# Six of the eight w_ob blocks ahead of the attention's combination, and the column sums of the second LayerNorm's mean in other stages

## The chip, the core and the metric

The kernel runs on one core of a Trainium2 chip. The metric is the device time of one execution in microseconds (us). Five engines take part. TensorE (PE in the profile; its weight loads are PEld) multiplies matrices. VectorE (DVE) and ScalarE (ACT) do the element-wise work and read the products out of PSUM. GpSimd (POOL) adds and subtracts weight matrices. SyncE (SP) issues almost all the DMAs. Each engine works through its own instructions in the order in which they stand in the program, and waits on semaphores for the others.

## What is computed

One layer of a decoder for 1024 prompt tokens and 32 sample tokens, 1056 columns in all. The part that matters here comes after the first feed-forward half-step and the first LayerNorm:

```python
z = h @ w_in + b_in
A = combine_groups(outs, lses)            # three groups of dilated attention, weighted by their softmax denominators
yb, vrows = sgu_branch(uv, ...)           # chunked spatial gating
mix = (sigmoid(ga) * (A @ w_oa) + sigmoid(gb) * (yb @ w_ob)) @ w_out
h = layer_norm(ALPHA * h + mix, ln2_g, ln2_b)
h = layer_norm(ALPHA * h + 0.5 * swiglu(h, ...), ln3_g, ln3_b)
```

Here ga and gb are the last 2 x 1024 columns of z: 16 blocks of 128, the gate blocks.

## The kernel before

Activations lie feature-major: a tile has 128 features on its partitions and columns of tokens, 264 in a chunk, four chunks (NC). A product in full fp32 precision is made of three passes over values split into a high and a low half, so each 128x128 weight block and chunk costs three matmuls of 128x264. The high half is a copy on ACT (L237), the low half a subtraction on DVE (L238); this holds for weights (tiles W) and activations (tiles S).

The kernel is written for one engine order by a scheduler that works from the order in which the Python code issues things. Long pieces of side work are generators in three queues, `bg`, `slow` and `mid`. After each block of matmuls the code calls `tick(n, m)`, which runs n steps of `bg`, m of `slow` and three of `mid`; `pause(n)` in a generator is n empty steps. So the code's ticks set how side work is spread among the blocks, and the scheduler's order fixes it for each engine.

The function `mix` (L1471 on) does the stage in question:

- Ten of the gate blocks (four chunks each, `gate8`, 24 matmuls per chunk). Each product leaves PSUM by an ACT activation into a tile M (L937) and is stored to the scratch zD in DRAM (L938). There are six M buffers for everything.
- Beside them, from `bg`, the six pairs of heads and groups (`attend`), one after the other: load q, k, v from zD (L1085), transpose v on PE (L1127) into V, scores (L1147), bias and minimum on DVE (L1155), exponential on ACT (L1159), transposes (L1170), values (L1186), and at its end a transpose of the row minima and sums (L1208), which go to DRAM as mlD. After the third and the sixth pair `combine` is put in `mid`: it reads mlD back, computes the weights of the three groups on 16 partitions (L1244 to L1257), writes them to cD, reads them back broadcast to 64 partitions (L1266), and multiplies and adds on DVE (L1271 to L1274).
- The spatial gating (`sgu_norm`, `sgu_mix`), from `mid`; its tiles vr are loaded from zD, transposed on PE (L1416) and normalized.
- The eight w_ob blocks (`local(n)`): per chunk 12 matmuls into one of the three PSUM banks named mm, then DVE multiplies the product into the gate tile mt[n], which was loaded from zD (L1488). Four of them stand before the loop that empties the queues, four among the next blocks.
- The eight w_oa blocks: per chunk 6 matmuls with the combined attention, DVE multiplies into ta[n] (L1488 again). Then DVE adds ta[n] to mt[n] (L1564), and the sum is split into m2[n] (L237, L238). The gates loaded late get their sigmoid here on ACT (L1495, L1560).
- `column_sums`, put in `bg` ahead of the w_oa blocks: it loads five w_out blocks into tiles Q (L1531), reduces them on DVE (L1533), and adds up hs, the part of the mean that comes from them, one 128x1056 multiply and seven multiply-adds (L1544, L1546), one as each mt[n] is finished.
- The w_out blocks (`block`, L1581): products of all eight m2 with w_out, 24 matmuls per chunk. The third block is followed by `center`, which subtracts the mean and uses hs (L527).

Of the kernel before, what the change touches and what calls it, by code (L numbers as in the profile page):

```python
# [22 lines left out]
KB = D // P  # L23
# [45 lines left out]
NLEAD = 6  # L69
NTAIL = 10  # L70
LAST = 4
CHUNKED = 3
SPLIT = [*QKV, 22, 23, 24, 25, 18, 19, 20, 21, *GATES[NLEAD : 16 - NTAIL]]
DENSE = GATES[:NLEAD] + GATES[16 - NTAIL :]
# [4 lines left out]
class Trunk:  # L79
# [705 lines left out]
    def out(self, w2, i, mode, ready, between, load):  # L785
# [84 lines left out]
        for c in range(NC):  # L870
            early = 6 if c == 0 else 0
            if mode != "out":
                self.hold_normed(c)
                if c == 2:
                    self.early = [self.unit(self.a["wzp"][n], slot=True, ahead=AFTER) for n in range(CHUNKED)]
            for n in range(KB):
# [153 lines left out]
    def widen(self):  # L1030
# [22 lines left out]
        for c in range(NC):  # L1053
            self.drain(lns.pop(c))
            if c == NC - 1:
                self.slow.append(self.spread(1, Y, self.A, nc.vector))
            for n in range(CHUNKED):
                self.gate8(units[n], DENSE[n], c, AF.Sigmoid, STEPS["lead"], 1)
        units = Y = None
        for n in range(CHUNKED, NLEAD):  # L1060
            w = self.unit(a["wzp"][n])
# [39 lines left out]
    def attend(self, i):  # L1101
# [11 lines left out]
        else:  # L1113
            nc.vector.memset(bias[:, :, :P], BIG)
            for h in range(2):
                b = bd[2 * hp + h]
                for r in range(2):
                    o = slice(64 * r, 64 * r + 64)
                    nc.sync.dma_start(bias[o, h, o], bass.AP(b.tensor, b.offset + 255, [[383, 64], [1, 64]]))
        yield from self.pause(2)  # L1120
        self.fetch_qkv(i + 1)
        V = self.Q([P, 8, P])
        for b in range(2):
# [347 lines left out]
    def mix(self):  # L1471
# [3 lines left out]
        def split_att():  # L1475
            for hp in range(2):
                h, l = self.S([P, NT], F32R), self.S([P, NT], F32R)
                for o in (slice(0, NP), slice(NP, NT)):
                    self.split(h[:, o], l[:, o], self.att[hp][:, o])
                att.append((h, l))  # L1480

        def product(wo, xs, c, t):
            p = self.mm_tile()[:, :C]
            cc = slice(c * C, c * C + C)
            for k, (xh, xl) in enumerate(xs):
                self.mm3(p, wo, k * P, xh[:, cc], xl[:, cc], k == 0, k == len(xs) - 1)
            with self.urgent():
                nc.vector.tensor_tensor(t[:, cc], t[:, cc], p, op=ALU.mult)  # L1488

        def local(n):  # L1490
            wb = self.unit(a["wo"][n, :, 2 * P :], 4 * P)
            if n + 2 < KB:
                mt[n + 2] = self.fetch_z(36 + n)
            if 34 + n in LATE_GATES:
                nc.scalar.activation(mt[n], mt[n], AF.Sigmoid)  # L1495
            for c in range(NC):
                product(wb, self.yb, c, mt[n])
                self.tick(STEPS["wob"], 1)
# [6 lines left out]
        self.bg.extend(self.attend(i) for i in range(len(HPG)))  # L1505
        for n in range(NLEAD, NLEAD + NTAIL - LAST):
            w = self.unit(a["wzp"][n])
            for c in (0, 2, 1, 3):
                self.gate8(w, DENSE[n], c, AF.Identity, STEPS["tail"], 1)
        units = {n: self.unit(a["wzp"][n]) for n in range(NLEAD + NTAIL - LAST, NLEAD + NTAIL)}  # L1510
        for c in range(NC):
# [4 lines left out]
            mt[n] = self.fetch_z(34 + n)  # L1516
        while any(g in self.mid for g in sgu):
            self.step(self.mid, 1)
        for n in range(KB // 2):
            local(n)  # L1520
        ta = [self.fetch_z(26 + n) for n in range(2)]
        while self.bg or self.mid or self.slow:
            self.tick(1, 1)
        split_att()
        done = 0

        def column_sums():
            wr, wsum = self.X([P, KB - half, KB], "wr", 1), self.X([P, KB], "wsum", 1)
            for q in range(KB - half):
                raw = self.Q([P, D])  # L1530
                nc.sync.dma_start(raw, a["wout"][half + q])  # L1531
                yield from self.pause()
                nc.vector.tensor_reduce(  # L1533
                    wr[:, q], raw.rearrange("p (k x) -> p k x", x=P), axis=AX.X, op=ALU.add
                )
            nc.vector.tensor_reduce(wsum, wr.rearrange("p q k -> p k q"), axis=AX.X, op=ALU.add)
            nc.vector.tensor_scalar(wsum, wsum, 1.0 / ALPHA, None, op0=ALU.mult)
            self.hs = self.S([P, NT])
            for n in range(KB):
                while done <= n:  # L1540
                    yield
                w = wsum[:, n : n + 1]
                if n == 0:
                    nc.vector.tensor_scalar(self.hs, mt[n], w, None, op0=ALU.mult)  # L1544
                else:
                    nc.vector.scalar_tensor_tensor(self.hs, mt[n], w, self.hs, op0=ALU.mult, op1=ALU.add)  # L1546
                yield

        half = 3
        sums = column_sums()  # L1550
        self.bg.append(sums)
        m2 = []
        for n in range(KB):
            wa = self.unit(a["wo"][n], 2 * P)
            if n + 2 < KB:
                ta.append(self.fetch_z(28 + n))
            if n < KB // 2:
                local(KB // 2 + n)
            if 26 + n in LATE_GATES:
                nc.scalar.activation(ta[n], ta[n], AF.Sigmoid)  # L1560
            for c in range(NC):
                product(wa, att, c, ta[n])
                self.tick(2)
            nc.vector.tensor_tensor(mt[n], mt[n], ta[n], op=ALU.add)  # L1564
            m2.append((self.S([P, NT], F32R), self.S([P, NT], F32R)))
            self.split(*m2[n], mt[n])
            done += 1
        self.yb = None
        self.sqs, self.lns = {}, {}
        self.drain(sums)  # L1570
        hs, self.hs = self.hs, None
        self.Y = self.new_Y(self.hD[0])

        def block(w, n, c):
            p = self.mm_tile()[:, :C]
            cc = slice(c * C, c * C + C)
            for k, (h, l) in enumerate(m2):
                self.mm3(p, w, k * P, h[:, cc], l[:, cc], k == 0, k == KB - 1)
            y = self.Y[c][n // KH][:, n % KH]
            with self.urgent():  # L1580
                nc.vector.scalar_tensor_tensor(y, p, 1.0 / ALPHA, y, op0=ALU.mult, op1=ALU.add)  # L1581
            if n >= half:
                self.square_step(c, n)
            self.tick(STEPS["wout"], 1)

        centers = []
        for n in range(half):
            w = self.unit(a["wout"][n])
            for c in range(NC):
                block(w, n, c)  # L1590
                if n == half - 1:
                    centers.append(self.center(c, hs, REST))
                    self.mid.append(centers[c])
        ws = [self.unit(a["wout"][n], slot=n < KB - 4) for n in range(half, KB)]
# [2 lines left out]
        for c in range(NC):  # L1597
# [7 lines left out]
            if c == 2:  # L1605
                units = [self.unit(a["w13b"][0, x], slot=True) for x in range(2)]
                self.drain(self.lns[1])
                self.slow.append(self.spread(0, self.Y, self.normed, nc.vector))
        hs = None
        self.A = self.normed  # L1610
        self.early = units, self.spread(1, self.Y, self.normed, nc.vector)

# [158 lines left out]
```

## Time and profile before

| | |
|---|---|
| median of 3 runs | 2224.24 us (2222.52 to 2227.31) |
| profiled execution, its own time | 2226.7 us |
| its span | 2224.9 us |
| mean granted TensorE clock | 0.984 |
| PE busy, PEld busy | 97%, 95% of the span |
| DVE, ACT, POOL busy | 70%, 40%, 15% |

The stage of the change runs from about 1060 to 1440 us in the span. In a timeline row the columns are start, length, engine, line, operation, tiles (output<-inputs), shape and count; in square brackets stands how long the engine was idle before it and what it waited for. A merged row covers several instructions that follow each other. PE's busy time counts a matmul that runs at a lower granted clock in full, so a slow stretch shows as a longer time per matmul and not as idle time.

### The profile page before, as it was taken

The numbers are of one execution on the slowest core, as the hardware profiler recorded it, in microseconds if no ns is written. First come the engines' busy times: TensorE is split into PE (matmuls) and PEld (weight loads), VectorE is DVE, ScalarE is ACT, GpSimd is POOL, SyncE is SP. The second block draws the span as 40 slices with busy tenths as digits, with TensorE's granted clock in tenths as the row PEclk, the third lists the DMA queues.
The fourth block names the chain that finished last, engine by engine and source line by source line (L and its number), as shares of the span: only waits on it lengthen the run. The fifth ranks groups of instructions, "written<-read, shape, count | busy, mean of one in ns | idle before, by whom it ended". The sixth has DMA issues, their size and how long they took to land.

```text
span 2224.9 us, 43158 instructions
## 1 busy us (share of the span) xinstructions
PE 2156.3 (97%) x17281; PEld 2104.8 (95%) x17281; DVE 1559.7 (70%) x2698; ACT 898.8 (40%) x1684; POOL 330.8 (15%) x238
## 2 busy tenths in 40 slices
PE   9999999999999999999899979998999999999997
PEld 8999999999999999999788868998999999999997
DVE  8776677656789537887485448678677676656687
ACT  5444444321126534434464533246444444421124
POOL 0433333100000013231000000100432332100000
PEclk9999999999999999999999989999999999999999
DMA  4445445597953236567664365513545545596831
GB/s 157 143 141 188 170 161 180 194 362 271 356 190 136 103 122 210 208 219 250 234 215 136 118 204 181 197 40 117 178 152 172 180 159 184 189 357 231 307 102 78
DMA packets 163640, 416.83 MB, mean 187 GB/s; under 512 B 24096, under 2 KB 60688, under 8 KB 160752
## 3 DMA queue, kind: packets, MB, share of 16 engines
q1 hardware_dynamic: 163008, 413.55, 53.0%
q8 instruction: 135, 2.21, 0.4%
q10 hardware_dynamic: 432, 0.54, 0.1%
q14 instruction: 65, 0.53, 0.1%
HBM read 301.64 MB, written 158.57 MB: 207 GB/s over the span
## 4 chain that ended last, share of the span: by engine, by line
PE 82%; DMA 6%; DVE 6%; ACT 2%; issue 2%; POOL 1%; SPq 1%; ACTq 0%; DVEq 0%; POOLq 0%
PE ax L226 43%; PE mm L226 35%; DMA M<-kv 2%; PE ax L1147 1%; DVE W L238 1%; DVE S L238 1%; PE ax L1170 1%; PE ax L1186 1%; DMA R<-wz 1%; DMA zD<-M 1%; DMA S<-zD 1%; DMA zD<-S 0%; DVE S L604 0%; DVE S L1488 0%; DVE M L1328 0%
## 5 line engine op out<-in xcount | busy, mean ns | idle before, releaser
L226 PE MATMUL mm<-S,W 128*128 128x264 f32 x5040 | 685.3, 291 | 38.4 <-DVE S L1488 23.0
L226 PE MATMUL ax<-S,W 128*128 128x264 f32 x5472 | 716.9, 285 | 0.3 <-ACT S L977 0.2
L226 PEld LDWEIGHTS mm<-S,W 128*128 128x128 f32 x5040 | 647.4, 193 | 55.4 <-DVE S L1488 19.6
L226 PEld LDWEIGHTS ax<-S,W 128*128 128x128 f32 x5472 | 685.5, 188 | 2.7 <-ACT S L977 1.3
L226 PE MATMUL ax<-S,S 128*128 128x264 f32 x3288 | 484.8, 285 | 1.6 <-DVE S L986 1.4
L226 PEld LDWEIGHTS ax<-S,S 128*128 128x128 f32 x3288 | 434.5, 188 | 3.5 <-DVE S L986 2.5
L226 PE MATMUL mm<-S,S 128*128 128x264 f32 x2496 | 391.7, 287 | 5.8 <-ACT S L237 3.3
L226 PEld LDWEIGHTS mm<-S,S 128*128 128x128 f32 x2496 | 341.0, 190 | 7.4 <-ACT S L237 3.5
L237 ACT CAST W<-R 128x256 fp32r<-128x256 f32 (+2 forms) x172 | 127.9, 759 | 369.7 <-PE mm L226 134.6
L368 POOL TENSOR_TENSOR Q<-R 128x512 f32<-128x512 f32 x50 | 71.0, 1420 | 792.3 <-DVE S L448 216.6
L238 DVE TENSOR_TENSOR W<-R,W 128x256 fp32r<-128x256 f32 (+2 forms) x172 | 148.4, 870 | 28.2 <-ACT W L237 27.8
L237 ACT CAST W<-Q 128x1024 fp32r<-128x1024 f32 (+1 forms) x79 | 77.8, 985 | 187.8 <-POOL Q L369 83.2
L443 DVE TENSOR_TENSOR S<-ax,M 128x264 f32<-128x264 f32 x84 | 33.8, 432 | 155.0 <-PE ax L226 154.6
L780 DVE SCALAR_TENSOR_TENSOR S<-ax,S 128x264 f32<-128x264 f32 x240 | 99.0, 427 | 58.5 <-PE ax L226 57.2
L105 POOL CAST S<-ones 128x1 fp32r<-128x1 f32 x32 | 19.2, 625 | 769.8 <-DVE S L238 613.5
L238 DVE TENSOR_TENSOR S<-Q,S 128x1024 fp32r<-128x1024 f32 (+2 forms) x87 | 124.8, 1434 | 7.1 <-ACT S L237 6.3
L237 ACT CAST S<-Q 128x1024 fp32r<-128x1024 f32 (+2 forms) x87 | 86.4, 993 | 102.0 <-PE ax L226 71.4
L238 DVE TENSOR_TENSOR W<-Q,W 128x1024 fp32r<-128x1024 f32 (+1 forms) x79 | 92.1, 1166 | 22.5 <-ACT W L237 22.5
L238 DVE TENSOR_TENSOR S<-S,M 128x528 fp32r<-128x528 f32 x72 | 83.8, 1164 | 3.9 <-ACT M L237 2.2
L369 POOL TENSOR_TENSOR Q<-Q,R 128x512 f32<-128x512 f32 x50 | 84.1, 1683 | 2.7
L376 POOL TENSOR_TENSOR Q<-R,Q 128x512 f32<-128x512 f32 x50 | 82.1, 1641 | 1.2
L237 ACT CAST S<-R 128x512 fp32r<-128x512 f32 (+1 forms) x65 | 44.4, 686 | 91.5 <-DMA sumsA<-S 37.9
(200 smaller groups left out, 2068.9 us busy)
## 6 DMA issues: line engine op xcount, KB each, us to landing
ws<-st SPq DMA_DIRECT2D x144, 256.0 KB
S<-sumsA SPq DMA_DIRECT2D x63, 528.0 KB
S<-sumsB SPq DMA_DIRECT2D x63, 528.0 KB
M<-kv SPq DMA_DIRECT2D x96, 256.0 KB
sumsA<-M SPq DMA_DIRECT2D x90, 264.0 KB
sumsB<-M SPq DMA_DIRECT2D x90, 264.0 KB
R<-w13b SPq DMA_DIRECT2D x44, 512.0 KB
S<-zD SPq DMA_DIRECT2D x42, 528.0 KB
```

The lines of the kernel that those rows point to most:

```text
L105: self.nc.gpsimd.tensor_copy(t[:, 0, :1] if len(shape) == 3 else t[:, :1], self.ones[:, :1])
L226: mm = lambda a, b, s, e: nc.tensor.matmul(o, a[:, cc], b, start=s, stop=e, skip_group_check=True)
L237: a = self.nc.scalar.copy(hi, src)
L238: b = self.nc.vector.tensor_tensor(lo, src, hi.bitcast(F32), op=ALU.subtract)
L368: tt(s12[:, lo], cd[:, lo], cd[:, hi], op=ALU.add)
L369: tt(s12[:, hi], s12[:, lo], ab[:, lo], op=ALU.subtract)
L376: tt(s34[:, hi], ab[:, hi], s12[:, hi], op=ALU.subtract)
L443: go(one, 5, False, lambda x: tt(h[:, x, 1], one[x], p7[:, x], op=ALU.add))
L780: nc.vector.scalar_tensor_tensor(y(x, r, e), bank[x], HALF, y(x, r, e), op0=ALU.mult, op1=ALU.add)
L1147: nc.tensor.matmul(pS[h][:, r, :nk], q[e, i * P : (i + 1) * P], k[e, k0 : k0 + nk], start=True, stop=True)
L1170: nc.tensor.transpose(pT[r][:, h, o], s[:, r, h, o], self.ident)
L1186: nc.tensor.matmul(pv[0][e, (i % 4) * P : (i % 4 + 1) * P], V[:, i - (nb - 1) + b, e], sT[:, r, h, b * P : b * P + P], start=b == 0, stop= ...
```

## The change

It does four things, all in `attend` and `mix`. The first pair of `attend` pauses eight steps instead of two before it transposes v. Six w_ob blocks, not four, are issued before the loop that empties the queues, and two among the w_oa blocks. `column_sums` moves from `bg` to `slow`, is put there ahead of the w_ob blocks, and starts hs only when all eight mt[n] are finished; each w_oa chunk ticks `slow` once and `bg` not at all. And hs is finished with the third w_out block instead of ahead of the first.

```diff
@@ attend
-        yield from self.pause(2)
+        yield from self.pause(2 if i else 8)
@@ mix
-        for n in range(KB // 2):
-            local(n)
-        ta = [self.fetch_z(26 + n) for n in range(2)]
-        while self.bg or self.mid or self.slow:
-            self.tick(1, 1)
-        split_att()
-        done = 0
-
         def column_sums():
...
             nc.vector.tensor_scalar(wsum, wsum, 1.0 / ALPHA, None, op0=ALU.mult)
+            while done < KB:
+                yield
             self.hs = self.S([P, NT])
             for n in range(KB):
-                while done <= n:
-                    yield
...
-        half = 3
+        done, half = 0, 3
         sums = column_sums()
-        self.bg.append(sums)
+        self.slow.append(sums)
+        for n in range(EARLY):
+            local(n)
+        ta = [self.fetch_z(26 + n) for n in range(2)]
+        while self.bg or self.mid or self.slow[0] is not sums:
+            self.tick(1, 1 if self.slow[0] is not sums else 0)
+        split_att()
...
-            if n < KB // 2:
-                local(KB // 2 + n)
+            if n < KB - EARLY:
+                local(EARLY + n)
...
                 product(wa, att, c, ta[n])
-                self.tick(2)
+                self.tick(0, 1)
...
-        self.drain(sums)
-        hs, self.hs = self.hs, None
...
                 if n == half - 1:
+                    while sums in self.slow:
+                        self.step(self.slow, 1)
+                    hs = self.hs
                     centers.append(self.center(c, hs, REST))
```

EARLY is 6 and KB is 8. The changed kernel has one line more near its top, so its L1209, L1272 and L1489 are L1208, L1271 and L1488 of before; `column_sums` and `block` move by other amounts (L1537 and L1539 are the old L1544 and L1546, L1579 the old L1581). On every engine the order of instructions is the same up to the first v transposes (on SP, up to the loads behind those for the first pair), and again from the third w_out block on.

The first place is PE at the end of the sixth pair of `attend`. Tiles mm are products: mm_15256 and mm_15288 are the last two gate chunks, mm_15333, mm_15351 and mm_15373 the first three chunks of the first w_ob block. L1208 (L1209) is the transpose with which `attend` ends. Before:

```order
L226 MATMUL mm_15256<-S_8412,W_14454 128x264
L226 MATMUL mm_15256<-S_8410,W_14455 128x264
L226 MATMUL mm_15288<-S_12644,W_14461 128x264
L226 MATMUL mm_15288<-S_12645,W_14461 128x264
L1170 MATMUL ax_15020<-ident,S_14966 128x128
L1208 MATMUL ax_15066<-ident,X_14816 32x128
L226 MATMUL mm_15288<-S_12644,W_14462 128x264
```

And in the changed kernel, where the first w_ob block is numbered alike:

```order
L1171 MATMUL ax_15085<-ident,S_15032 128x128
L227 MATMUL mm_15373<-S_13440,W_15325 128x264
L227 MATMUL mm_15373<-S_13439,W_15326 128x264
L227 MATMUL mm_15373<-S_13552,W_15325 128x264
L1171 MATMUL ax_15086<-ident,S_15032 128x128
L1209 MATMUL ax_15132<-ident,X_14882 32x128
L227 MATMUL mm_15373<-S_13553,W_15325 128x264
```

The transpose moves from the beginning of the last gate chunk to the third chunk of the first w_ob block, 50 products of L226 later on PE; between it and the first product into mm_15387, the fourth w_ob chunk, stand 58 products before and 8 now.

The second place is DVE at the second combination. S_15109 (S_15175) are the 16-partition weights, S_15142 to S_15144 (S_15208 to S_15210) their broadcast, and S_15320 is mt[0], the gate tile of the first w_ob block. Before:

```order
L1257 TENSOR_TENSOR S_15109<-X_15122,S_15109 16x128 x3
L1271 TENSOR_TENSOR S_15141<-S_14096,S_15142 128x1024
L1273 TENSOR_TENSOR S_14496<-S_14496,S_15143 128x1024
L1274 TENSOR_TENSOR S_15141<-S_15141,S_14496 128x1024
L1273 TENSOR_TENSOR S_14817<-S_14817,S_15144 128x1024
L1488 TENSOR_TENSOR S_15320<-S_15320,mm_15333 128x264
L1488 TENSOR_TENSOR S_15320<-S_15320,mm_15351 128x264
L1488 TENSOR_TENSOR S_15320<-S_15320,mm_15373 128x264
```

Now:

```order
L1258 TENSOR_TENSOR S_15175<-X_15188,S_15175 16x128 x3
L1272 TENSOR_TENSOR S_15207<-S_14166,S_15208 128x1024
L1274 TENSOR_TENSOR S_14560<-S_14560,S_15209 128x1024
L1275 TENSOR_TENSOR S_15207<-S_15207,S_14560 128x1024
L1274 TENSOR_TENSOR S_14883<-S_14883,S_15210 128x1024
L1489 TENSOR_TENSOR S_15320<-S_15320,mm_15333 128x264
L1489 TENSOR_TENSOR S_15320<-S_15320,mm_15351 128x264
L1489 TENSOR_TENSOR S_15320<-S_15320,mm_15373 128x264
```

Nothing moves here: in both kernels the first three w_ob products leave PSUM behind the combination's multiplications.

The third place is DVE among the last w_oa blocks. S_15408 and S_15486 are mt[3] and mt[4], S_15883 and S_15995 (S_16006 and S_16056) are ta tiles, S_15869 is hs and W tiles are weights. Before:

```order
L1564 TENSOR_TENSOR S_15408<-S_15408,S_15760 128x1056
L1488 TENSOR_TENSOR S_15883<-S_15883,mm_16110 128x264
L1488 TENSOR_TENSOR S_15883<-S_15883,mm_16119 128x264
L1546 SCALAR_TENSOR_TENSOR S_15869<-S_15408,X_15664,S_15869 128x1056
L1488 TENSOR_TENSOR S_15883<-S_15883,mm_16127 128x264
L238 TENSOR_TENSOR S_16097<-S_15408,S_16096 128x1056
L1488 TENSOR_TENSOR S_15883<-S_15883,mm_16135 128x264
L1488 TENSOR_TENSOR S_15995<-S_15995,mm_16158 128x264
L238 TENSOR_TENSOR W_16307<-R_16305,W_16306 128x1024
```

Now, from the addition for the same mt[3] on:

```order
L1564 TENSOR_TENSOR S_15408<-S_15408,S_15892 128x1056
L1489 TENSOR_TENSOR S_16006<-S_16006,mm_16122 128x264
L1489 TENSOR_TENSOR S_16006<-S_16006,mm_16130 128x264
L1489 TENSOR_TENSOR S_16056<-S_16056,mm_16153 128x264
L239 TENSOR_TENSOR W_16298<-R_16296,W_16297 128x1024
L1564 TENSOR_TENSOR S_15486<-S_15486,S_16006 128x1056
L1489 TENSOR_TENSOR S_16056<-S_16056,mm_16161 128x264
L239 TENSOR_TENSOR S_16093<-S_15408,S_16092 128x1056
```

The multiply-add into hs (L1546) is gone from here; all eight instructions of hs now stand behind the first w_out product's L1579.

More of the change, by code (lines that the diff above doesn't have):

```diff
@@ L71 @@
 LAST = 4
+EARLY = 6
 CHUNKED = 3
@@ L1608, in mix @@
                 self.slow.append(self.spread(0, self.Y, self.normed, nc.vector))
-        hs = None
+        hs = self.hs = None
         self.A = self.normed
```

## The prediction

> **What bounds the kernel now.** I read the page's busy times first, then PE's waits in the stage that the change touches, then the timelines of PE and DVE there.
>
> ```profile
> PE 2156.3 (97%) x17281; PEld 2104.8 (95%) x17281; DVE 1559.7 (70%) x2698; ACT 898.8 (40%) x1684; POOL 330.8 (15%) x238
> PE 82%; DMA 6%; DVE 6%; ACT 2%; issue 2%; POOL 1%; SPq 1%; ACTq 0%; DVEq 0%; POOLq 0%
> ```
>
> PE carries the kernel and its work is not changed, so the time can move only by PE's waits and by stretches in which it runs slowly after them. Between 1060 and 1560 us PE waited for these, most first (total, times, longest):
>
> ```profile
> PE mm L226 <- DVE S L1488: 23.0, 11, 14.9
> PE mm L226 <- ACT M L937: 6.1, 3, 3.7
> ...
> PE ax L1127 <- DMA S<-zD: 5.5, 1, 5.5
> ...
> PE ax L1127 <- DVE X L1466: 1.2, 1, 1.2
> ```
>
> The timeline of PE has them in place:
>
> ```profile
> 1058.26 7.71 PE L226 MATMUL mm<-S,W 128*128 128x264 f32 x62
> 1071.47 1.97 PE L1127 MATMUL ax<-ident,S 128*128 128x128 f32 x8 [5.50 <-DMA S<-zD]
> 1073.37 1.66 PE L1147 MATMUL ax<-S,S 64*128 64x128 f32 x8
> 1074.96 4.97 PE L226 MATMUL mm<-S,W 128*128 128x264 f32 x28
> 1081.37 4.76 PE L226 MATMUL mm<-S,W 128*128 128x264 f32 x37 [1.44 <-ACT M L937]
> ...
> 1215.34 5.21 PE L226 MATMUL mm<-S,W 128*128 128x264 f32 x22 [3.68 <-ACT M L937]
> ...
> 1296.23 0.27 PE L1208 MATMUL ax<-ident,X 128*32 128x128 f32 x1
> ...
> 1300.30 4.39 PE L226 MATMUL mm<-S,W 128*128 128x264 f32 x34
> 1319.58 27.58 PE L226 MATMUL mm<-S,W 128*128 128x264 f32 x210 [14.89 <-DVE S L1488]
> ...
> 1396.03 4.30 PE L226 MATMUL mm<-S,W 128*128 128x264 f32 x18 [3.00 <-DVE S L1488]
> 1401.66 18.62 PE L226 MATMUL mm<-S,W 128*128 128x264 f32 x134 [1.33 <-DVE S L1488]
> ```
>
> An undisturbed product costs 0.123 us, by a piece of the chain of waits behind this stage (28.37/231):
>
> ```profile
> 1413.18 28.37 PE mm L226 x231
> ```
>
> The longest wait, 14.89 us, is for DVE to free a PSUM bank, and DVE's timeline says why it was late:
>
> ```profile
> 1306.15 0.87 DVE L1257 TENSOR_TENSOR S<-X,S 16x128 f32<-16x128 f32 x3
> 1313.31 1.23 DVE L1271 TENSOR_TENSOR S<-S,S 128x1024 f32<-128x1024 f32 x1 [6.29 <-DMA S<-cD]
> ...
> 1317.93 1.22 DVE L1273 TENSOR_TENSOR S<-S,S 128x1024 f32<-128x1024 f32 x1
> 1319.10 1.11 DVE L1488 TENSOR_TENSOR S<-S,mm 128x264 f32<-128x264 f32 x3
> ```
>
> The first w_ob products wait in the three banks behind the whole combination: its small operations, the way through DRAM and its multiplications. So PE's restart hangs on the last L1208: from 1296.23 to 1319.58 is 23.35 us, whatever PE does meanwhile. Behind it DVE becomes the bound of the w_oa blocks, in this table by stretch (PE, PEld, DVE, ACT and POOL busy, granted clock, DMA share and rate):
>
> ```profile
> 1060.00:1080.00 20.00, 14.43 (x94) 13.03 (x92) 8.12 (x19) 3.96 (x8) 0.00 (x0) 0.83 0.95 335
> ...
> 1349.00:1382.00 33.00, 30.46 (x231) 29.89 (x232) 28.54 (x54) 12.37 (x17) 0.00 (x0) 0.95 0.65 212
> 1382.00:1413.00 31.00, 25.09 (x161) 23.29 (x160) 28.11 (x36) 12.43 (x12) 7.82 (x10) 0.83 0.58 202
> ```
>
> In the last stretch PE issues 161 products, 19.8 us of work, in 31 us, while DVE does not rest until 1409.85.
>
> **The change, part by part.** *The six blocks ahead of the combination.* They would fill the 14.89 us if their products could leave PSUM. They can't: in both orders DVE's first three L1488 stand behind the combination's last L1273, so PE stops at the fourth w_ob chunk as before, and four or six blocks ahead make no difference there. I take 0 for it.
>
> *The longer pause.* Every later step of the attention slides back against the gate blocks. Up to the last L1208 PE now has 50 more products to do, and between it and the stop 8 instead of 58. The 23.35 us behind L1208 stay, since nothing in that chain is removed; the restart therefore comes 50 x 0.123 = 6.1 us later, and the wait grows from 14.9 to about 21.5 us. This is a loss of **6.1 us**, unless waits ahead of L1208 become shorter.
>
> *The first of these waits.* The pause should move the transposes behind the arrival of v. It moves the whole set in the code, but in the order the first four still stand only 4 products later, and the load of v has kept its place in SP's queue. PE will stop there for 5.5 - 4 x 0.123 = 5.0 us. Four transposes and the scores follow later. The next stop is the one before 1081.37: a bank waits for ACT's L937, which waits for the store of an earlier M tile.
>
> ```profile
> 1072.83 7.27 DMA zD<-M
> ...
> S<-zD SPq DMA_DIRECT2D x42, 528.0 KB
> ...
> S<-wsT SPq DMA_DIRECT2D x1, 256.0 KB
> S<-sgu_b SPq DMA_DIRECT2D x1, 256.0 KB
> ```
>
> Ahead of that store SP now has one zD load less than three, and the loads of wsT and sgu_b in their place: 1056 - 512 = 544 KB fewer, 1.7 us at the 335 GB/s of the stretch. So PE goes on at about 1079.7, with up to 2.6 us still to do that was done before (half of the 1.97 us of transposes and the 1.66 us of scores, at that stretch's low clock; at full clock about half). That is -0.4 to +0.9 us. PE now waits some 3 us there, not 1.44, and may restart slowly: the row at 1396.03 had 18 products in 4.30 us after 3.00 us, 2.1 us too many. Ends -0.4 and +3.0; I take **+1 us**, between them, since the wait is nearest to the 1396 one but the products are fewer. The Trainium skill, "TensorE: Matmul & The Clock Gate", Part 1, says that the clock falls back after an idle window of about 3.4 us; by that rule this shorter wait would cost no slow start, the term would be about 0 and the forecast 2223.5 us. The row at 1396.03 speaks against it, though short waits ahead of it may have added up.
>
> *The other waits of the gate stage* (6.1 us less the 1.44, another 1.2 us ahead of transposes, and the slow restart of 22 products at 1215.34: 5.21 - 2.7 = 2.5 us). The stop at 1215 has the gate stores behind the broadcast of the first combination in SP's queue; now M_14465's store stands ahead of the cD stores and M_14504's behind, as M_14313's and M_14375's did. I take 0, with ends of -6.2 (the stop gone) and +6.2 (one more like it).
>
> *The sums out of the w_oa blocks.* Two loads of work leave DVE where it is the bound. What each costs there is seen by the starts in its timeline:
>
> ```profile
> 1361.41 1.21 DVE L1533 TENSOR_REDUCE X<-Q 128x8 f32<-128x1024 f32 x1
> 1362.54 0.68 DVE L238 TENSOR_TENSOR W<-R,W 128x512 fp32r<-128x512 f32 x1
> ...
> 1366.27 0.76 DVE L1544 TENSOR_SCALAR S<-S,X 128x1056 f32<-128x1056 f32 x1
> 1366.95 0.42 DVE L238 TENSOR_TENSOR W<-R,W 128x256 fp32r<-128x256 f32 x1
> ...
> 1396.48 1.22 DVE L238 TENSOR_TENSOR W<-R,W 128x1024 fp32r<-128x1024 f32 x1
> 1397.62 1.31 DVE L1546 SCALAR_TENSOR_TENSOR S<-S,X,S 128x1056 f32<-128x1056 f32 x1
> 1398.85 1.25 DVE L238 TENSOR_TENSOR S<-S,S 128x1056 fp32r<-128x1056 f32 x1
> 1400.01 1.25 DVE L1564 TENSOR_TENSOR S<-S,S 128x1056 f32<-128x1056 f32 x1
> 1401.18 1.10 DVE L1488 TENSOR_TENSOR S<-S,mm 128x264 f32<-128x264 f32 x3
> ...
> 1404.60 0.42 DVE L1488 TENSOR_TENSOR S<-S,mm 128x264 f32<-128x264 f32 x1
> ...
> 1408.60 1.25 DVE L238 TENSOR_TENSOR S<-S,S 128x1056 fp32r<-128x1056 f32 x1
> ```
>
> From start to start: a reduction 1.13 us, the first hs instruction 0.68, a weight split of 1024 1.14, a multiply-add 1.23, a split or an addition of 1056 1.17, an L1488 0.34. Before, the last L1488 ends at 1404.94, 85.4 us after the restart. Now PE has six blocks and two pairs first, 4 x 48 + 2 x 48 + 2 x 72 - 36 = 396 products with the three done ones taken off, 48.6 us, and the slow restart (27.58 - 210 x 0.123 = 1.8 us): 50.4. DVE has some 34 us to do until then, by the same starts. Six w_oa blocks without w_ob follow, 17.7 us for PE, but for DVE up to the last L1489 24 x 0.34 + 6 additions and 5 splits x 1.17 + one reduction 1.1 and two very short ones, taken as 0.3, + two weight splits of 256, 0.8, + three of 1024 x 1.14 = 26.7 us, behind the 0.7 us of the first product. That ends at 77.8, or 78.6 with 0.8 us for casts that come late on ACT. The gain is 85.4 - 78.6 = **6.8 us**. It can't exceed by much the eight hs instructions, 7 x 1.23 + 0.7 = 9.3; and it shrinks to about 3 if the last ta tiles, which now have 8 us between the SP load and their use, come late. What covers the hs work now: it stands among the first eight w_out chunks, each 24 x 0.123 = 2.9 us on PE, so DVE has 23 us there for 9.3 of hs, 8 evictions and 4 weight splits, some 17 us. Without that cover it would cost the 9.3 back.
>
> **Sum**: +6.1 + 1 + 0 - 6.8 = +0.3 us. On the profiled execution's 2226.7 us that is 2227.0; the median of the runs is 2224.24, so I forecast **2224.5 us**, no change that can be told: a measurement of this kernel separates about 0.2%, 4.4 us.
>
> **The rivals.** *Slower: the gate stores come late.* SP now issues six zD loads (two for the second pair, four vr) ahead of the store of the second gate tile; before it was far ahead of the vr loads. That is 6 x 528 KB, 9.7 us at 335 GB/s, and there are six M buffers, three of them slabs. If that store lands after about 1092, when PE's next bank needs the buffer, PE stops; a stop such as at 1215.34 costs 3.7 + 2.5 = 6.2 us. Against it: I count five buffers free in time. With a second one, or with the last ta late as well, the time is 2224.5 + 6 to 10, about 2232.
>
> *Faster: the gate stage's waits fall away.* The attention now runs against other gate chunks, and the stops at 1215 and around 1155 are accidents of the order. Without the first, 2224.5 - 6.2 = 2218; for it speaks that one more gate store goes ahead of the combination, against it that a single M tile is left there for gates in both.
>
> *The filling works after all*: if mt[0] and the evictions ran ahead of the combination, two more blocks would fill 96 x 0.123 = 11.8 us: about 2212. The order of DVE excludes it.
>
> *The pause does what it says*: v there in time, 5.0 us of wait and the 3 us of slow work behind it (28 products in 4.97 us and transposes) gone: 2217. The kept place of the first four transposes excludes all but a remainder.
>
> **How the numbers follow.** No change 0.37; slower rival 0.35; faster by the gate waits 0.24, by the last two together 0.04. The ends of the terms (-6 to +6 for the gate waits, -0.4 to +3, gain of 3 to 9.3) seldom meet on one side; I put the range from 2215 to 2236, which reaches into both rivals and leaves out about 2 in 10. Within 0.2% I give 0.37, faster 0.28, slower 0.35.
>
> **What would show it.** In the profile after: a stop of about 5 us before the first L1128; the last L1209 about 6 us later than 1296.2, or less by what the gate waits give; PE's wait for L1489 about 21.5 us; 23 us from L1209 to the restart; the end of the last L1489 some 78.6 us after the restart, not 85.4; no wait of PE for hs among the w_out blocks. It is wrong if the wait for L1489 is short, if waits for L938 add up to far more or less than 6 us, or if DVE is late in the w_out blocks.

## The result and the profile after

The changed kernel takes 2225.55 us in the median of 12 runs (2223.16 to 2230.03), the kernel before 2225.73 us on the same chip (12 runs, 2222.03 to 2228.81). The ratio is 1.0002 with a 95% interval of 0.9993 to 1.0011: no change that can be told, as forecast (2224.5 us). The profiled execution after has a span of 2223.3 us. The zero is a loss and a gain of some 7 to 9 us each, which the traces and the experiments show apart.

The page of the changed kernel (busy times), and PE's waits between 1060 and 1560 us in its trace (total, times, longest):

```profile
PE 2148.0 (97%) x17281; PEld 2095.8 (94%) x17281; DVE 1560.7 (70%) x2698; ACT 898.6 (40%) x1684; POOL 327.1 (15%) x238
```

```profile
PE mm L227 <- DVE S L1489: 27.9, 9, 20.9
PE mm L227 <- ACT M L938: 6.3, 3, 2.9
...
PE ax L1171 <- ACT S L1160: 2.7, 2, 2.6
PE ax L1128 <- DMA S<-zD: 1.8, 1, 1.8
PE ax L1148 <- DVE M L1467: 1.2, 1, 1.2
```

The longest wait has grown from 14.9 to 20.9 us, the wait for v has shrunk from 5.5 to 1.8, and the gate stage has new waits at L1171 and L1148. The timeline of PE after has them in place:

```profile
1070.86 0.66 PE L1128 MATMUL ax<-ident,S 128*128 128x128 f32 x4 [1.75 <-DMA S<-zD]
1071.27 3.14 PE L227 MATMUL mm<-S,W 128*128 128x264 f32 x24
1077.35 7.36 PE L227 MATMUL mm<-S,W 128*128 128x264 f32 x46 [2.94 <-ACT M L938]
...
1132.10 0.33 PE L1171 MATMUL ax<-ident,S 128*128 128x128 f32 x1 [2.56 <-ACT S L1160]
...
1305.57 0.27 PE L1209 MATMUL ax<-ident,X 128*32 128x128 f32 x1
...
1328.29 24.53 PE L227 MATMUL mm<-S,W 128*128 128x264 f32 x189 [20.88 <-DVE S L1489]
...
1400.61 2.45 PE L227 MATMUL mm<-S,W 128*128 128x264 f32 x18 [2.43 <-DVE S L1489]
...
1406.03 35.76 PE L227 MATMUL mm<-S,W 128*128 128x264 f32 x288 [0.17 <-DVE S L1489]
1441.62 1.98 PE L227 MATMUL mm<-S,S 128*128 128x264 f32 x15
```

The last of these rows is the start of the fourth w_out block, the first with a weight kept in a tile S. Before, its row was

```profile
1439.56 2.00 PE L226 MATMUL mm<-S,S 128*128 128x264 f32 x15
```

DVE's timeline after, at the combination, at the end of the w_oa blocks, and where hs now stands:

```profile
1315.45 0.87 DVE L1258 TENSOR_TENSOR S<-X,S 16x128 f32<-16x128 f32 x3
1321.89 1.23 DVE L1272 TENSOR_TENSOR S<-S,S 128x1024 f32<-128x1024 f32 x1 [5.58 <-DMA S<-cD]
...
1326.67 1.23 DVE L1274 TENSOR_TENSOR S<-S,S 128x1024 f32<-128x1024 f32 x1
1327.81 1.10 DVE L1489 TENSOR_TENSOR S<-S,mm 128x264 f32<-128x264 f32 x3
...
1406.96 0.76 DVE L1489 TENSOR_TENSOR S<-S,mm 128x264 f32<-128x264 f32 x2
...
1414.93 0.76 DVE L1537 TENSOR_SCALAR S<-S,X 128x1056 f32<-128x1056 f32 x1
...
1430.43 1.31 DVE L1539 SCALAR_TENSOR_TENSOR S<-S,X,S 128x1056 f32<-128x1056 f32 x1
```

Three places serve as marks in every kernel below: V, the first transpose of v for the first pair; T, the last transpose of `attend` (L1208 or L1209); and W, the start of the fourth w_out block. From V to T the changed kernel takes 234.7 us (1305.57 - 1070.86), the kernel before 224.8; from T to W 136.1 us against 143.3. So the loss lies ahead of T, the gain behind it.

### The profile page after: what moved, and what is told of

It reads as the page before. It is cut to its first block, busy times and chain, and to the rows that moved or that the text cites. A ratio compares the mean times of both kernels' runs of the same rounds, so it can differ in the third digit from the quotient of the medians.

```text
span 2223.3 us, 43147 instructions
## 1 busy us (share of the span) xinstructions
PE 2148.0 (97%) x17281; PEld 2095.8 (94%) x17281; DVE 1560.7 (70%) x2698; ACT 898.6 (40%) x1684; POOL 327.1 (15%) x238
## 5 line engine op out<-in xcount | busy, mean ns | idle before, releaser
L227 PE MATMUL mm<-S,W 128*128 128x264 f32 x5040 | 677.4, 289 | 43.3 <-DVE S L1489 27.9
L227 PEld LDWEIGHTS mm<-S,W 128*128 128x128 f32 x5040 | 640.5, 191 | 59.7 <-DVE S L1489 28.1
L239 DVE TENSOR_TENSOR S<-Q,S 128x1024 fp32r<-128x1024 f32 (+2 forms) x87 | 125.7, 1445 | 6.5 <-ACT S L238 5.6
```

The source lines that it names most:

```text
L227: mm = lambda a, b, s, e: nc.tensor.matmul(o, a[:, cc], b, start=s, stop=e, skip_group_check=True)
L239: b = self.nc.vector.tensor_tensor(lo, src, hi.bitcast(F32), op=ALU.subtract)
```

## The experiments

Each ratio is to the kernel before on the same chip in the same session, with its 95% interval; 0.001 is 2.2 us. In the diffs the base is the kernel before, or where it says so another one.

### The pause alone, and all but the pause

The first kernel is the kernel before with the longer pause:

```diff
-        yield from self.pause(2)
+        yield from self.pause(2 if i else 8)
```

> The kernel before with the longer pause of the first pair alone. On PE the last transpose of attend then stands 50 products later, as in the changed kernel. My theory (nothing in the 23 us between that transpose and the restart is removed, so the restart slides back with it): 50 x 0.123 = 6.1 us slower plus at most 1 for the gate stage, 2230 to 2233 us where the kernel before takes 2225 (ratio 1.0025 to 1.0035); PE's longest wait for L1488 grows from 14.9 to about 21 us. Rival (the pause pays for itself, since the waits for v and for M tiles in the gate stage fall away by as much): within 1.5 us of before (ratio 1.000), and then the sums bring nothing either.

Measured: 2231.56 us (2227.97 to 2235.19), ratio 1.0041 (1.0028 to 1.0055), 9 us slower. The second is the changed kernel with the opposite edit, six blocks ahead and the sums moved:

> The changed kernel with the short pause back: six blocks ahead and the sums moved. My theory: 5 to 7 us faster than before (ratio 0.997 to 0.9975, some 2219 us), with the longest wait for L1489 at about 15 us again, and the last L1489 some 79 us behind the restart. Rival (the sums are not worth what I said, and the pause costs nothing): as before within 1.5 us.

Measured: 2215.44 us (2212.26 to 2218.43), ratio 0.9967 (0.9955 to 0.9979), 7.3 us faster. PE's timeline with the pause alone:

```profile
1074.42 0.66 PE L1127 MATMUL ax<-ident,S 128*128 128x128 f32 x4 [1.50 <-DMA S<-zD]
...
1309.16 0.27 PE L1208 MATMUL ax<-ident,X 128*32 128x128 f32 x1
1332.10 23.02 PE L226 MATMUL mm<-S,W 128*128 128x264 f32 x169 [21.10 <-DVE S L1488]
```

and without it:

```profile
1071.77 1.75 PE L1128 MATMUL ax<-ident,S 128*128 128x128 f32 x8 [1.89 <-DMA S<-zD]
...
1294.62 0.27 PE L1209 MATMUL ax<-ident,X 128*32 128x128 f32 x1
1317.88 29.01 PE L227 MATMUL mm<-S,W 128*128 128x264 f32 x225 [14.80 <-DVE S L1489]
...
1430.93 1.98 PE L227 MATMUL mm<-S,S 128*128 128x264 f32 x15
```

From T to the restart it is 22.9 us with the pause and 23.3 without: the chain doesn't care when it starts, and the restart slides with T. From V to T the two differ by 234.74 - 222.85 = 11.9 us. Four of the 50 products stand ahead of V, and the other 46 account for 5.7 us of it. Single executions vary here: V to T is 231.2 to 234.7 us in the four profiled with the long pause, and 220.1 to 224.8 in the ten with the short one. From T to W the pause alone takes 141.5 us, 1.9 less than before. The runs show 9.1 +/- 3 us in all. The theory holds; the pause is perhaps dearer than the 7.1 us that I had at most, but the interval doesn't exclude them.

### The six blocks alone, and the sums alone

The kernel before with six blocks ahead:

```diff
+EARLY = 6
...
-        for n in range(KB // 2):
+        for n in range(EARLY):
             local(n)
...
-            if n < KB // 2:
-                local(KB // 2 + n)
+            if n < KB - EARLY:
+                local(EARLY + n)
```

> The kernel before with six w_ob blocks ahead of the combination and nothing else changed; hs and the reductions stay among the w_oa blocks. My theory: 0 within 1.5 us (ratio 0.9995 to 1.0005), since DVE still has the combination ahead of the first three evictions, and the work of DVE among the blocks is the same in sum; the longest wait stays at about 15 us. Rival (the two more blocks fill the wait, or spread DVE's work better): 3 us or more faster (ratio under 0.9985).

Measured: 2226.11 us (2220.18 to 2231.57), ratio 1.0013 (1.0002 to 1.0024), 2.9 us slower: neither. The changed kernel with the short pause and `EARLY = 4`, so that only the sums are moved:

> The sums moved as in the changed kernel, but four w_ob blocks ahead as before, and the short pause. What was measured so far: six blocks and sums together -7.3 us, six blocks alone +2.9 us. Theory A (the six blocks press DVE's work into six w_oa blocks without w_ob work for PE, whatever lies in the queues; the sums' removal is worth its DVE work alone): this is faster than the six-block version, by about 3 us, 10 us faster than before (ratio 0.9955). Theory B (the six blocks do harm only while the sums are among the w_oa blocks): the same as the six-block version within 1.5 us (ratio 0.9967).

Measured: 2218.81 us (2215.78 to 2224.13), ratio 0.9983 (0.9971 to 0.9995), 3.8 us faster. Theory A called for 10 and falls. Theory B called for the 7.3 of the six-block version; the ratios of the two versions differ by 3.6 us, 3.8 either way, and can't settle it alone. The traces speak against it. From T to W it is 143.3 and 143.5 us in the two profiled executions of the kernel before, 147.1 with six blocks alone, 139.8 with the sums alone and 136.3 with both, each of these in one execution. So the two edits don't add: by the ratios +2.9 and -3.8 apart, -7.3 together, and from T to W some +3.7 and -3.6 apart, -7.1 together. Busy times from the restart to the last L1488 (L1489) of the w_oa blocks, and for the first two kernels in 25 us of it as well, in the order stretch, its length, PE, PEld, DVE, ACT, POOL, granted clock, DMA share and rate. Before:

```profile
1345.00:1370.00 25.00, 22.79 (x181) 21.97 (x180) 22.51 (x45) 9.64 (x14) 0.00 (x0) 1.00 0.66 212
...
1319.50:1405.10 85.60, 76.80 (x550) 74.29 (x551) 69.51 (x129) 33.17 (x40) 4.01 (x7) 0.90 0.63 223
```

Six blocks alone:

```profile
1345.00:1370.00 25.00, 23.86 (x194) 23.37 (x192) 19.49 (x39) 6.07 (x10) 0.00 (x0) 1.00 0.50 163
...
1316.10:1403.50 87.40, 76.19 (x563) 74.12 (x564) 70.03 (x128) 32.72 (x40) 4.24 (x7) 0.92 0.61 217
```

The sums alone:

```profile
1322.40:1403.40 81.00, 73.51 (x554) 70.83 (x555) 61.54 (x121) 32.79 (x40) 0.98 (x1) 0.96 0.66 236
```

Both, without the pause:

```profile
1317.80:1397.20 79.40, 71.72 (x555) 69.50 (x556) 60.99 (x120) 31.19 (x39) 0.18 (x1) 0.98 0.65 231
```

The sums take 8 to 8.5 us of DVE's work out of the stretch, and the stretch gets 4.6 us shorter with four blocks ahead, 6.2 (both edits against neither) with six. The six blocks alone lengthen it by 1.8 us, and PE then waits once more, at the w_out blocks, where DVE in turn waits for a load of h, which the first w_out evictions need:

```profile
1412.05 13.20 PE L227 MATMUL mm<-S,W 128*128 128x264 f32 x94 [2.20 <-DVE S L1582]
```

```profile
1411.57 0.43 DVE L1582 SCALAR_TENSOR_TENSOR S<-mm,S 128x264 f32<-128x264 f32 x1 [3.25 <-DMA S<-hD]
```

In the chain of waits this load starts at 1405.96, behind a w_out weight in SP's queue that goes out at 1404.65, just after DVE has split an earlier weight; DVE's lateness reaches PE on this way too. So the order of the blocks is not free behind the restart. With the sums still in `bg`, six blocks ahead leave DVE less to do early (19.5 of 25 us busy from 1345 on, 22.5 before), since the reductions and hs come with the w_oa blocks; they then stand against six blocks with little for PE to do. That this is why six blocks alone cost time fits the table, but no run shows it apart. Why six blocks are no harm, and rather a help, once the sums are gone is not settled either. Three differences to the sums alone can be seen: PE's waits in the stretch are shorter, 2.4 us at most instead of 3.5; its mean granted clock there is higher (0.98 against 0.96); and a wait of 1.4 us at the first w_out products, for the load of h again, is gone.

### The kernel before once more

> The kernel before again, for a second profiled execution. Three executions with the same instructions up to the first v transposes waited 1.6 to 2.0 us for v there, the profile of before 5.5 us. Theory (the 5.5 us belonged to that one execution, in which PE came to the place some 4 us earlier than the load of v): a wait of about 2 us, and from the last widening row at 1055 to the last L1208 some 236 us, not 241. Rival (the wait is a property of the kernel before): 5 us again.

Measured: a wait for v of 2.7 us, and 222.8 us from V to T (before: 224.8). From the start of the last widening row (1054.98 before, 1060.50 here) to T it is 236.5 us, where the first execution took 241.2.

```profile
1074.21 1.09 PE L1127 MATMUL ax<-ident,S 128*128 128x128 f32 x8 [2.73 <-DMA S<-zD]
```

The versions with the short pause, which are the same up to there, show everything from no wait to 6.7 us; the two ends are the sums moved alone, and the second version with early gate tiles (below):

```profile
1076.48 1.97 PE L1128 MATMUL ax<-ident,S 128*128 128x128 f32 x8 [6.74 <-DMA S<-zD]
```

```profile
1063.96 1.03 PE L1128 MATMUL ax<-ident,S 128*128 128x128 f32 x8
```

The theory holds: the 5.5 us belonged to that one execution.

### Seven of the eight hs instructions left out

The base is the changed kernel:

```diff
-                else:
-                    nc.vector.scalar_tensor_tensor(self.hs, mt[n], w, self.hs, op0=ALU.mult, op1=ALU.add)
```

> The changed kernel with seven of the eight hs instructions left out, the multiply-adds of 1.23 us each, so that the mean of the second LayerNorm lacks seven eighths of its w_out part. Theory (they are covered by the first eight w_out chunks, in which DVE has 23 us for 17 us of work): as the changed kernel, within 1.5 us (ratio to before 0.9995 to 1.001). Rival (they only moved the bound by one stage): 4 to 8 us faster than before.

Measured: 2226.08 us (2222.06 to 2229.27), ratio 1.0011 (1.0000 to 1.0023), no faster than with them. In the changed kernel PE ran the 288 products of 1406.03 in 35.76 us, 0.124 each, while DVE did all eight. The cover is there, and the rival falls.

### The evictions ahead of the combination

If the long wait is there because the first evictions stand behind the combination on DVE, it must go when they stand ahead. The base is the changed kernel with the short pause. The gate tiles are fetched earlier, three ahead instead of two, and the second combination is delayed:

```diff
@@ combine
+        if hp:
+            yield from self.pause(15)
         raw = self.S([16, 3, 2, P])
...
-        yield
+        yield from self.pause(6 if hp else 1)
...
-        yield from self.pause(3)
+        yield from self.pause(12 if hp else 3)
@@ mix
-            if n + 2 < KB:
-                mt[n + 2] = self.fetch_z(36 + n)
+            if n + 3 < KB:
+                mt[n + 3] = self.fetch_z(37 + n)
...
         for c in range(NC):
+            if c == NC - 1:
+                for n in range(3):
+                    mt[n] = self.fetch_z(34 + n)
             for n in units:
...
-        for n in range(2):
-            mt[n] = self.fetch_z(34 + n)
```

> The kernel with the short pause, six blocks ahead and the sums moved, in which the first three gate tiles mt are fetched ahead of the last four gate chunks, and the second combination starts later (pauses of 15, 6 and 12 steps before its loads, its small operations and its multiplications). In DVE's order the first twelve evictions then stand ahead of the combination's multiplications. My theory (the long wait is there only since the first evictions stand behind the combination): PE's wait of 15 us for L1489 falls under 3, with the slow start of 1.8 us behind it; some 12 to 16 us faster than the same kernel without the early evictions, and 17 to 22 us faster than before (2204 to 2209 us). Rival (the chain through DRAM is only pushed to the w_oa blocks, which then wait for the split of the combined attention): PE waits 5 to 12 us at the first w_oa product in place of it, and the kernel is 7 to 13 us faster than before.

Measured: 2209.39 us (2207.36 to 2211.53), ratio 0.9939 (0.9926 to 0.9952), 13.6 us faster than before. Its longest wait for an eviction (here L1491) is 3.9 us:

```profile
1292.50 0.27 PE L1209 MATMUL ax<-ident,X 128*32 128x128 f32 x1
...
1324.44 35.60 PE L227 MATMUL mm<-S,W 128*128 128x264 f32 x270 [3.92 <-DVE S L1491]
...
1424.34 1.97 PE L227 MATMUL mm<-S,S 128*128 128x264 f32 x15
```

DVE's timeline tells what that wait is, the broadcast weights (L1276 is the multiplication by them):

```profile
1321.36 1.23 DVE L1276 TENSOR_TENSOR S<-S,S 128x1024 f32<-128x1024 f32 x1 [4.50 <-DMA S<-cD]
```

The cause of the long wait is shown: it goes when the first evictions stand ahead of the combination. But the edit moves two things for that, DVE's order and the loads of the gate tiles. In the kernel before, SP's queue holds these loads back too; its eight zD loads of this place, six gate tiles mt and two ta, follow the loads of the broadcast weights:

```profile
1308.44 3.66 SPq L1266 DMA_DIRECT2D S<-cD  x6
1312.14 5.93 SPq L1085 DMA_DIRECT2D S<-zD  x8
```

With the edit the first three gate tiles are issued at 1291.36, ahead of T. So another order on DVE alone would still have left the first evictions, at 1319.10 in that kernel, without their gate tile until some time after 1312.14. No run has one of the two without the other. The size is between the theories. From T to W it is 131.8 us, 4.5 less than without the early evictions, though a wait of 14.8 us is gone. Busy times from T to W without the early evictions, and with them (columns as above):

```profile
1294.62:1430.93 136.31, 113.87 (x899) 110.58 (x896) 97.84 (x172) 41.14 (x52) 4.38 (x10) 0.95 0.65 225
```

```profile
1292.50:1424.34 131.84, 118.64 (x898) 114.96 (x896) 96.01 (x172) 38.49 (x50) 5.43 (x10) 0.95 0.67 232
```

PE idles 9.2 us less (22.4 to 13.2), but the same products keep it busy 4.8 us longer. The mean clock of the stretch is the same, but it counts the waits too, and in the long wait without the early evictions it is low (0.65 from 1303.1 to 1317.8). The shorter waits are followed by more slow work: with the early evictions 25 products take 5.56 us from 1324.44 on, at a granted clock of 0.50, and 36 take 5.71 us from 1387.29 on, at 0.65 to 0.75, together 3.8 us more than at 0.123 each. Without them there is one such place, 46 products in 7.12 us from 1317.88 on, 1.5 us too many. That is about half of the 4.8 us; the rest is open. Now the same with the long pause:

> The early gate tiles and the delayed combination (13.6 us faster than before), now with the pause of eight steps. Theory (6 us of the pause's price come from the restart that hangs on the last transpose of attend; with the evictions ahead of the combination nothing hangs on it): the pause costs only the waits in the gate stage, 3 to 6 us, ratio to before 0.9955 to 0.9965. Rival (the pause costs its 8 to 9 us whatever stands behind it): ratio 0.9975 to 0.998.

Measured: 2210.24 us (2206.32 to 2213.56), ratio 0.9939 (0.9921 to 0.9957). The pause costs 0 us here, 5 either way, rather less than the 3 to 6 of the theory; the rival's 8 to 9 us are excluded:

```profile
1302.86 0.27 PE L1209 MATMUL ax<-ident,X 128*32 128x128 f32 x1
...
1422.89 1.98 PE L227 MATMUL mm<-S,S 128*128 128x264 f32 x15
```

V to T is 9.1 us longer than with the short pause (231.2 against 222.1), T to W 11.8 us shorter (120.0). Of these, 6.1 us are the 50 products, which are done ahead of T. So the pause's price, or most of it, is the restart that hangs on T. That the gate stage's own waits come back as well is seen in these two traces, and its cause is open.

### Which blocks, and how late

The multiplications later, with pauses of 18 and 24 in place of 15 and 12:

> The early gate tiles again, with longer pauses in the second combination (18 steps before its loads, 24 before its multiplications), so that the multiplications stand behind 18 evictions of w_ob products and not behind 12; there PE had waited 3.9 us while DVE waited for the broadcast weights. Theory: that wait goes, 2 to 5 us faster than with the shorter pauses, ratio to before 0.9915 to 0.993. Rival (DVE, which is the bound of the w_oa blocks, only takes the same time later): ratio 0.994 as before it.

Measured: 2205.52 us (2199.97 to 2208.88), ratio 0.9916 (0.9898 to 0.9934). The ratio is the theory's, 5 us less than with the shorter pauses, 5 either way. But the wait doesn't go: PE's longest wait for an eviction is still 2.9 us, and so is DVE's for the broadcast weights. And with four blocks ahead, at pauses of 15 and 12:

```diff
-EARLY = 6
+EARLY = 4
```

> The early gate tiles and the delayed combination (ratio 0.9939 with six blocks ahead), with four w_ob blocks ahead. Theory (once the evictions run ahead of the combination, the blocks ahead are what fills the 23 us and the split of the combined attention behind them; four blocks are 23.6 us of products and run out first): PE waits 3 to 6 us at the first w_oa product, and with the 3 us that four blocks cost with the sums moved it is 4 to 9 us slower than with six, ratio to before 0.996 to 0.998. Rival (four blocks are enough): 0.994.

Measured: 2201.79 us (2198.83 to 2208.03) where the kernel before takes 2225.48 us, ratio 0.9898 (0.9879 to 0.9916), 23 us faster than before and the fastest version of all. My theory falls, and the code says why: `local(EARLY + n)` stands ahead of the w_oa block n, so that with four blocks "ahead" the fifth is issued before the first w_oa product too. Five blocks are 240 products, 29.5 us. So four are enough; why they are 9 us better than six (5 either way), while with the stop in place they were no better, no run settles. PE's longest stop for an eviction is now 2.7 us:

```profile
1292.24 0.27 PE L1209 MATMUL ax<-ident,X 128*32 128x128 f32 x1
...
1376.13 3.44 PE L227 MATMUL mm<-S,W 128*128 128x264 f32 x18 [2.72 <-DVE S L1491]
...
1417.93 1.99 PE L227 MATMUL mm<-S,S 128*128 128x264 f32 x15
```

T to W is 125.7 us. Longer pauses (18 and 18) with four blocks go too far:

> Four blocks ahead, the sums moved, the early gate tiles, and pauses of 18, 6 and 18 steps in the second combination where 15, 6 and 12 gave a ratio of 0.9898. The multiplications then stand 13 evictions back, not 12, on DVE, and the small operations one chunk later. Theory (there the wait for the broadcast weights is only 2.3 us of PE): 1 to 2 us faster, ratio 0.989. Rival (the combination is needed by the first w_oa product sooner than that and PE waits there): 1 to 4 us slower, 0.990 to 0.9915.

Measured: 2205.87 us (2201.73 to 2210.67), ratio 0.9928 (0.9912 to 0.9943), slower than 0.9898 as the rival said, by 6.7 us (5 either way) where it said 1 to 4, and at another place. PE stops 3.3 us for an eviction behind the first multiplication, and DVE waits 5.6 us there for the broadcast weights. Counted from T, the small operations end 0.8 us later than with the shorter pauses (18.9 against 18.1 us), but the first multiplication comes 4.2 us later (29.6 against 25.3); what holds the weights up beyond the later loads is open.

```profile
1324.32 1.69 PE L227 MATMUL mm<-S,W 128*128 128x264 f32 x12 [3.31 <-DVE S L1491]
```

```profile
1322.61 1.23 DVE L1276 TENSOR_TENSOR S<-S,S 128x1024 f32<-128x1024 f32 x1 [5.62 <-DMA S<-cD]
```

Last, the early evictions alone, on the kernel before (four blocks, sums in `bg`):

> The kernel before with the early gate tiles and the delayed combination alone: short pause, four blocks ahead, hs and the reductions among the w_oa blocks as before. With the sums moved as well the ratio was 0.9898. Theory (the early evictions take away the 15 us stop whatever else is done, and the sums are worth there what they were worth without them, 0.9983): ratio about 0.9915, with no wait of PE over 4 us between 1290 and 1440. Rival (with the stop gone DVE is the bound of more of the stage, and the sums weigh their full 9 to 15 us of DVE work): ratio 0.994 to 0.9965.

Measured: 2209.77 us (2206.91 to 2213.07), ratio 0.9948 (0.9934 to 0.9962), 11.6 us faster. Here the rival's ratio is right: moving the sums is worth 0.9948 - 0.9898 = 0.005, 11 us (5 us either way), once the stop is gone, against 3.8 us (2.7 either way) with it. The traces show the same direction, but less of it: from T to W the sums take off 5.8 us without the stop (131.5 to 125.7) and 3.6 us with it (143.4 to 139.8). That DVE's work weighs more once PE no longer stands still for another reason is therefore likely, and not shown.

## Why the prediction was right, point by point

- *The six blocks ahead, 0.* Right on the stop: it stays at 14.9 us with six blocks alone, since the order on DVE forbids them to leave PSUM. Wrong as a whole: alone they cost 2.9 us (0.4 to 5.3), and the trace has the loss behind the restart, 1.8 us in the stretch of the w_oa blocks and 2.2 at the first w_out products, which wait for a late load. The step looked at the stop only.
- *The longer pause, +6.1.* The mechanism is shown: T comes 50 products later, the 23 us behind it stay (22.7 after), the wait became 20.9 us (forecast 21.5). T itself stands at 1305.57, 9.3 us later than before and not 6: in this execution PE comes 2.7 us later into the stage, waits 3.7 us less for v, and loses more in the gate stage (next point). And when the restart no longer hangs on T, the pause costs 0 us, 5 either way.
- *The first wait, +1, and the other gate waits, 0.* These were too small. From V to T the changed kernel loses 11.9 us against the one without the pause, 6.2 more than its 46 more products: PE idles 11.9 us there instead of 7.7, and the other 2 us are slow work. The wait for the M tile before 1077.35 is 2.94 us and its 46 products take 7.36 us, 1.7 too many: some 3 us, the upper end given. The rest are new waits, 2.56 us for L1160 above all, which the forecast put at 0 within 6.2. By the runs the pause costs less than that, 9.1 us alone and 7.8 in the changed kernel (1.0002 / 0.9967), each within 3 us; the forecast's three terms make 7.1. The Trainium skill, "TensorE: Matmul & The Clock Gate", Part 1, would with its idle window of about 3.4 us have had no slow restart after 2.94 us; this row, at a granted clock of 0.77, is against it.
- *The v load, a stop of about 5 us.* Wrong: 1.75 us, but for no reason of the change that the traces show. With the short pause it varies from 0 to 6.7 us between executions of the same order; I took one execution's wait for a property of the kernel.
- *The sums, -6.8.* The last L1489 ends at 1407.72, 79.4 us behind the restart (forecast 78.6, before 85.4), and hs is hidden. But the term was booked to the sums alone, and it belongs to both edits: apart they are -3.8 and +2.9, together -7.3.
- *The sum, +0.3.* Forecast were +7.1 for the pause and -6.8 for the rest; measured are +7.8 and -7.3, each within 3 us, and -1.6 to +2.4 us for the whole. Both groups hold. Within the second, the two edits' own prices were wrong, and the error doesn't show because they came together and the 78.6 us were worked out for both. Within the first there is some luck: the traces lose more ahead of T than the forecast had, and where the runs get a part of it back is open.
- *The rivals.* The slower one (gate stores late) did not come. Of the faster ones, the stop at 1215 did shrink (1.5 us, at 1227.70), but others took its place (1.9 us at 1153.58, 2.6 at 1132.10). That filling is excluded by DVE's order was right, though the gate tiles came too late for it as well. The version that changes both on the kernel before shows what that was worth: 11.6 us.

## What to carry to other kernels

Work put ahead of a wait fills it only if its results can leave: look on the evicting engine for what stands ahead of them, and in the DMA queue for the tiles that they read, and move both, before adding more work. A delay of a step costs by what hangs on its last instruction; find that instruction first. Edits that touch the same bound need not add, and a wait for a transfer in one profiled execution is no property of the kernel until a second one shows it.

## What was unexpected in the hardware

PE's slow restart sets in below the 3 us that I had rows for, and not at one length of idle time. After a wait of 2.43 us, 18 products took 2.45 us (row 1400.61 after), close to 18 x 0.123 = 2.2. After 2.72 us they took 3.44 (row 1376.13 with four blocks and early evictions; granted clock 0.65), after 3.00 us 4.30 (row 1396.03 before; 0.50). So a wait of 2.7 us cost 1.2 us more than itself, one of 3.0 us 2.1 us more, and one of 2.4 us 0.2.

But shorter waits were followed by slow work too. With the early evictions and the long pause PE waited 2.25 us for v, with no wait in the row ahead:

```profile
1071.63 1.11 PE L1128 MATMUL ax<-ident,S 128*128 128x128 f32 x4 [2.25 <-DMA S<-zD]
1072.39 4.26 PE L227 MATMUL mm<-S,W 128*128 128x264 f32 x24
```

These four transposes and 24 products took 5.0 us at a granted clock of 0.68; in the changed kernel, after 1.75 us, the same took 3.6. And with four blocks and early evictions, 37 products after a wait of 2.2 us took 4.77 us at a clock of 1.00 with the shorter pauses (from 1078.06 on), and 6.29 us at 0.73 with the longer ones (from 1076.46 on). Two short waits close together are no clearer: after 1.72 and 0.95 us 19 products took 4.10 us (1156.81, without the pause), after 1.54 and 0.96 us 4.11 (1155.25, four blocks with the longer pauses), but after 1.56 and 0.96 us only 2.56 (1155.39, the early evictions alone). So no length of idle time in these runs separates slow from fast; what decides is open.
